# Value products evicted to SBUF in one step, their low half on GpSimd, one rotation buffer and convolution statistics one chunk earlier, in a two-layer decoder trunk

## The chip, the cores and the metric

The kernel runs on one core of a Trainium2 chip. The metric is the time of one execution on the device in microseconds. Before the change it is 650.95 us, the median of three runs (650.80, 650.95 and 651.51). The changed kernel is to be timed in the same way.

## What is computed

Two layers (DEPTH = 2) act on x of 256 positions by 1024 channels. In each layer one wide projection feeds a convolution branch and an attention branch. With one block of 256 keys the block-sparse attention is plain causal attention over 16 heads of 64.

```
u = x @ w_in + b_in
a_val, a_glu, a_z, q, k, v, b_z, g_a, g_b = jnp.split(u, SPLIT_POINTS, axis=-1)
h   = causal_depthwise_conv31(a_val * sigmoid(a_glu)) + conv_b
y_a = ((silu(layer_norm(h, cln_g, cln_b)) @ w_pw2) * silu(a_z)) @ w_proj_a
o   = softmax(causal(rope(q) / 8 @ rope(k).T)) @ v
y_b = (o * silu(b_z)) @ w_proj_b
out = (sigmoid(g_a) * y_a + sigmoid(g_b) * y_b) @ w_out
x   = layer_norm(ALPHA * x + out, ln_g, ln_b)
```

## The kernel before

**Numbers in two halves.** Every matrix and activation is kept as a high half (a rounded copy, written by ScalarE) and a low half (the rest, a subtraction). A product is high x high + high x low + low x high. All activations lie with channels on the partitions and the 256 positions along the free axis, except v and the last projection.

**The weight stream.** `STREAM` lists 52 weight tiles of 1 MB for each layer, in the order V, A_GLU and A_VAL by turns, B_Z, then the attention stage MID (Q, K, G_A by turns, then G_B), then A_Z, PB, PW2, PA, WO; each name has four tiles. `split_w` loads a tile (SP's queue), has ACT write its high half (line 120, four pieces) and POOL its low half (line 124, four pieces; a few tiles go to DVE). Raw, high and low tiles have three buffers each, and two tiles are prepared ahead.

**A gemm.** `gemm_a` uses one weight tile for two output chunks of 128 channels. A chunk is 8 matmuls of 512 columns (line 176: high weights on high and low activations side by side) and 8 of 256 columns (line 174: low weights). PSUM has three such buffers ("mm"). A chunk leaves by an ACT copy of the low product (`lw`, line 182 or 184), a DVE addition (line 187) and the evacuation that belongs to the projection. The order on PE is written out by hand (`manual_schedule`) in MID, A_Z and PB; a scheduler sets the order on the other engines, and in PW2 and PA on PE too. Where `gemm_a` calls a hook inside a chunk, it does so after its eighth matmul.

**Attention, in MID.** The rotation (`rope`, lines 429 to 440) is four DVE instructions for each Q or K tile. A pair p of heads (0 to 7) goes through three steps that hooks place between the matmuls of later gemms:

- `att_scores`: scores into one PSUM tile s (line 451), mask and maxima on DVE (457 to 459), exponentials on ACT (461 and 464), the reciprocal on DVE (466), the scaling on ACT (468 writes p0, 469 writes p1).
- `att_trans`: six transposes on PE into two PSUM tiles of the pool `ptp`, ta and tb (lines 477, 478, 479). The pool has two buffers, so that ta of pair p takes the buffer of ta of pair p-1, and tb that of tb. ACT copies them out (482, 483).
- `att_av`: the value product is written into the free half of tb (lines 491, 494). Then, lines 495 to 498:

```
g = ps[:, :S]
nc.vector.scalar_tensor_tensor(g, g, bias(V, p), bz[:, p, :], op0=ALU.add, op1=ALU.mult)
nc.scalar.activation(og[:, p, :], g, AF.Copy)
nc.vector.tensor_tensor(ol[:, p, :], g, og[:, p, :].bitcast(F32), op=ALU.subtract)
```

Here g is still the PSUM tile tb: DVE adds the bias and multiplies by the gate in place, ACT writes the high half, DVE the low half, and only then is tb free for the next pair's line 479.

**Convolution.** 31 taps for each of 8 channel tiles run on DVE in the background (line 381), some after every gemm chunk (`background`); line 386 sums the tiles for the mean. Its layer norm is placed by the constants `CM`, `CV` and `CB`: `hook_az` calls `cln_mu` after chunk `CM` of A_Z (matmul of line 542 on PE, subtraction 545, squares 546); `ev_pb` calls `cln_var` after chunk `CV` of PB (the sums 533 to 535, matmul 551, then the reciprocal root 554 to 559), and after chunk ct the tiles in `CB[ct]` go through `cln_b` (564 to 568), which writes hc, the input of PW2.

Of the kernel before, what the change touches and what calls it, by code (L numbers as in the profile page):

```python
# [10 lines left out]
F32 = mybir.dt.float32  # L11
# [4 lines left out]
ALU = mybir.AluOpType  # L16
# [4 lines left out]
S = 256  # L21
D = 1024
P = 128
# [8 lines left out]
NEG = -1e30  # L32
EARLY = 6
NH2 = 2
CM = 5.0
CV = 1
CB = [[], [], [0, 1], [2, 3], [4, 5], [6, 7], [], []]
KE = 7
KN = 5
L1, L2, L3 = 2.5, 5.5, 7.0  # L40
# [8 lines left out]
A_VAL, A_GLU, A_Z, Q, K, V, B_Z, G_A, G_B, PW2, PA, PB, WO = range(13)  # L49
# [21 lines left out]
def decoder_trunk(ctx: ExitStack, tc: tile.TileContext, a, out):  # L71
    nc = tc.nc
# [8 lines left out]
    tmp = ctx.enter_context(tc.tile_pool(name="tmp", bufs=2))  # L81
# [6 lines left out]
    def u_f32(name, shape=(P, KT, S)):  # L88
        return unit.tile(list(shape), F32, tag="u", name=name)

    def u_pair(name):

        both = pair.tile([P, KT, 2, S], F32R, tag="p", name=name)
        return both[:, :, 0, :], both[:, :, 1, :], both
# [51 lines left out]
    def background(n):  # L146
        with tc.high_priority(offset=-LATE):
            for _ in range(min(n, len(conv_ops))):
                conv_ops.pop(0)()
# [153 lines left out]
    for l in range(DEPTH):  # L303
# [3 lines left out]
        def bias(b, ct):  # L307
            return pc[:, b * KT + ct : b * KT + ct + 1]
# [104 lines left out]
        bz = u_f32(f"bz{l}")  # L413
# [9 lines left out]
        og, ol, op_ = u_pair(f"og{l}")  # L423
        qk = {}

        def ev_qk(b):
            return lambda j, ps: rope(b, j, ps)

        def rope(b, j, ps):
            u = tmp.tile([P, 2, S], F32, tag="t1", bufs=2, name=f"u_{l}_{b}_{j}")  # L430
            t2 = tmp.tile([P, 2, S], F32, tag="t2", bufs=1, name=f"t2_{l}_{b}_{j}")
            r0 = 2 if b == Q else 0
            cosb = rt[:, r0 : r0 + 1, :].to_broadcast([P, 2, S])
            sinb = rt[:, r0 + 1 : r0 + 2, :].to_broadcast([P, 2, S])
            nc.vector.tensor_tensor(u, ps, sinb, op=ALU.mult)
            nc.vector.stream_shuffle(t2, u, SWAP)
            nc.vector.tensor_tensor(ps, ps, cosb, op=ALU.mult)
            r = tmp.tile([P, 2, S], F32, tag="qk", bufs=4, name=f"r_{l}_{b}_{j}")
            nc.vector.tensor_tensor(r, ps, t2, op=ALU.add)
            qk[b, j] = r  # L440
# [45 lines left out]
        def att_av(p):  # L486
            pa, pb, tb = st[p]
            ps = tb[:, 2:, :].rearrange("p a q -> p (a q)")
            for e in range(2):
                hs = slice(p * P + e * HD, p * P + e * HD + HD)  # L490
                nc.tensor.matmul(ps[e * HD : e * HD + HD, :S], v[:, 0, hs], pa[:, e, :], start=True, stop=False)  # L491
            for e in range(2):
                hs = slice(p * P + e * HD, p * P + e * HD + HD)
                nc.tensor.matmul(ps[e * HD : e * HD + HD, P:S], v[:, 1, hs], pb[:, e, :], start=False, stop=True)
            g = ps[:, :S]
            nc.vector.scalar_tensor_tensor(g, g, bias(V, p), bz[:, p, :], op0=ALU.add, op1=ALU.mult)
            nc.scalar.activation(og[:, p, :], g, AF.Copy)
            nc.vector.tensor_tensor(ol[:, p, :], g, og[:, p, :].bitcast(F32), op=ALU.subtract)

        def ev_gate(b, dst):  # L500
            def f(ct, o):
# [5 lines left out]
        for n, (b, j) in enumerate(MID):  # L507
            if b == K:
                at = 2 * n + 1
                for p in (2 * j, 2 * j + 1):  # L510
                    for d, f in ((L1, att_scores), (L2, att_trans), (L3, att_av)):
                        plan.setdefault(at + d, []).append((f, p))
                    at += 3
# [34 lines left out]
        def cln_var():  # L548
            f = fold(cln["sq"], cln["sq"])
            vp = cvp.tile([P, 2, S], F32, tag="cv", name=f"cvar{l}")  # L550
            nc.tensor.matmul(vp[:, 0, :], ones, f, start=True, stop=True)
            u = tmp.tile([P, S], F32, tag="g", bufs=2, name=f"cu{l}")
            y = vp[:, 1, :]
            nc.scalar.activation(u, vp[:, 0, :], AF.Sqrt, bias=eps)
            nc.vector.reciprocal(y, u)
            nc.scalar.activation(u, y, AF.Square)
            nc.vector.tensor_scalar(vp[:, 0, :], vp[:, 0, :], EPS, None, op0=ALU.add)
            nc.vector.scalar_tensor_tensor(u, u, -0.5, vp[:, 0, :], op0=ALU.mult, op1=ALU.mult)
            nc.vector.scalar_tensor_tensor(y, u, 1.5, y, op0=ALU.add, op1=ALU.mult)
            cln["r"] = y  # L560

        def cln_b(ct):
            z = ptp.tile([P, 512], F32, tag="pt", name=f"z{l}_{ct}")[:, :S]
            nc.vector.tensor_tensor(z, cv[:, ct, :], cln["r"], op=ALU.mult)
            nc.scalar.activation(z, z, AF.Silu, bias=pc[:, C_LB + ct : C_LB + ct + 1],  # L565
                                 scale=pc[:, C_LG + ct : C_LG + ct + 1])
            nc.scalar.activation(hc[0][:, ct, :], z, AF.Copy)
            nc.vector.tensor_tensor(hc[1][:, ct, :], z, hc[0][:, ct, :].bitcast(F32), op=ALU.subtract)

        def ev_pb(ct, o):  # L570
            nc.vector.scalar_tensor_tensor(gb[:, ct, :], gb[:, ct, :], 1.0, o, op0=ALU.add, op1=ALU.mult)  # L571
            if ct == CV:
                hc.extend(u_pair(f"hc{l}"))
                cln_var()
            for q in CB[ct]:
                cln_b(q)

        def hook_az(c, j):
            if 2 * j + c == CM:
                background(len(conv_ops))  # L580
                cln_mu()
# [22 lines left out]
        mh, ml, _ = u_pair(f"mg{l}")  # L604
# [166 lines left out]
```

## Time and profile before

| | before |
|---|---|
| median of three runs | 650.95 us |
| the profiled execution | 650.61 us |
| its span, first to last instruction | 648.8 us |
| PE (matmuls) busy | 633.8 us |
| DVE busy | 485.3 us |
| ACT busy | 438.4 us |
| POOL busy | 487.6 us |
| granted TensorE clock, mean | 0.997 |

The profiled execution is 1.8 us longer than its span, and 0.34 us shorter than the median. PE is TensorE's matmuls, PEld its weight loads, DVE VectorE, ACT ScalarE, POOL GpSimd, SP the engine that issues the weight loads from HBM. A PE that is busy all the time can still lose time: the ends of its matmuls are modelled and overlap, so the distance between two starts tells more than the busy time.

### The profile page before, as it was taken

The page shows a single profiled execution, that of the slowest core. Times are in us where ns is not written, and L with a number is a line of the kernel's source. Part 1 is how long each engine was busy: PE and PEld are TensorE (multiplying, and loading weights), DVE is VectorE, ACT ScalarE, POOL GpSimd, SP SyncE. Part 2 cuts the span into 40 slices and gives each one's busy share as a digit, 9 for nine tenths or more (in the row PEclk, how much of TensorE's full clock was granted, in tenths as well). Part 3 has the DMA queues.
Part 4 walks back from the last instruction along what each step waited for, and adds up shares of the span by engine and source line. Part 5 has one row for each costly group of instructions (what it writes and reads, how often), then busy time and mean ns, then how long its engine had stood idle before and what let it go on. Part 6 is the DMA issues. An engine that isn't in the chain of part 4 may idle for free.

```text
span 648.8 us, 10605 instructions
## 1 busy us (share of the span) xinstructions
PE 633.8 (98%) x3662; PEld 542.2 (84%) x3662; DVE 485.3 (75%) x1129; ACT 438.4 (68%) x1019; POOL 487.6 (75%) x387
## 2 busy tenths in 40 slices
PE   8999999999999999999999999999999999999995
PEld 6888888887878888988788888888877888889884
DVE  4668989999998666445840899899999886664556
ACT  4675665887778689656527566668777787885641
POOL 0099999777566898989628999996677589999851
PEclk9999999999999999999999999999999999999998
DMA  8966555443333564555653555554433344555401
GB/s 272 351 235 251 190 196 195 162 162 131 131 129 131 195 250 155 201 179 195 254 195 116 209 195 204 191 190 154 173 131 130 130 146 179 195 186 191 175 33 66
DMA packets 19191, 116.06 MB, mean 179 GB/s; under 512 B 2113, under 2 KB 3393, under 8 KB 6209
## 3 DMA queue, kind: packets, MB, share of 16 engines
q1 hardware_dynamic: 18416, 114.72, 49.2%
q10 hardware_dynamic: 720, 0.66, 0.4%
q8 instruction: 29, 0.48, 0.3%
q14 instruction: 26, 0.20, 0.1%
HBM read 114.32 MB, written 1.05 MB: 178 GB/s over the span
## 4 chain that ended last, share of the span: by engine, by line
PE 83%; ACT 7%; DVE 4%; DMA 3%; POOL 1%; issue 1%; POOLq 0%; ACTq 0%
PE mm L176 43%; PE mm L174 23%; PE wo L210 3%; PE v L210 3%; ACT hi L120 3%; PE v L340 3%; PE s L451 2%; PE mm L171 2%; DMA raw<-w 1%; DMA xf<-xT 1%; PE tb L491 1%; POOL lo L124 1%; ACT z L565 1%; PE tb L479 1%; ACT s L461 1%
## 5 line engine op out<-in xcount | busy, mean ns | idle before, releaser
L124 POOL TENSOR_TENSOR lo<-raw,hi 128x512 fp32r<-128x512 f32 x380 | 485.8, 1315 | 138.4 <-ACT hi L120 133.6
L176 PE MATMUL mm<-x,hi 128*128 128x512 f32 x1024 | 263.8, 395 | 0.0
L120 ACT ACTIVATE hi<-raw 128x512 fp32r<-128x512 f32 x412 | 235.7, 629 | 23.3 <-DMA raw<-w 15.5
L176 PEld LDWEIGHTS mm<-x,hi 128*128 128x128 f32 x1024 | 184.0, 189 | 34.4 <-issue 2.4
L381 DVE SCALAR_TENSOR_TENSOR cv<-h,pc,cv 128x256 f32<-128x256 f32 x464 | 196.4, 481 | 0.2
L174 PEld LDWEIGHTS mm<-x,lo 128*128 128x128 f32 x1024 | 139.5, 190 | 11.2
L174 PE MATMUL mm<-x,lo 128*128 128x256 f32 x1024 | 147.5, 284 | 0.0
L187 DVE TENSOR_TENSOR mm<-mm,lw 128x256 f32<-128x256 f32 x172 | 73.5, 430 | 80.6 <-ACT lw L182 51.7
L182 ACT ACTIVATE lw<-mm,pc 128x256 f32<-128x256 f32 x128 | 61.4, 480 | 86.5 <-PE mm L176 86.3
L176 PE MATMUL mm<-og,hi 128*128 128x512 f32 x128 | 33.1, 396 | 0.0
L210 PE MATMUL wo<-hi,mg 128*128 128x512 f32 (+1 forms) x144 | 32.7, 368 | 0.1
L176 PE MATMUL mm<-ah,hi 128*128 128x512 f32 x128 | 32.4, 393 | 0.0
L124 DVE TENSOR_TENSOR lo<-raw,hi 128x512 fp32r<-128x512 f32 x32 | 25.6, 844 | 7.4 <-ACT hi L120 7.4
L210 PEld LDWEIGHTS wo<-hi,mg 128*128 128x128 f32 x144 | 25.2, 189 | 5.2 <-DVE mg L610 0.9
L184 ACT ACTIVATE lw<-mm 128x256 f32<-128x256 f32 x44 | 16.8, 386 | 16.7 <-PE mm L176 15.8
L176 PEld LDWEIGHTS mm<-og,hi 128*128 128x128 f32 x128 | 23.3, 189 | 4.1
L176 PEld LDWEIGHTS mm<-ah,hi 128*128 128x128 f32 x128 | 23.1, 189 | 4.0
L176 PE MATMUL mm<-hc,hi 128*128 128x512 f32 x96 | 25.1, 397 | 0.5 <-DVE gb L571 0.5
L176 PEld LDWEIGHTS mm<-hc,hi 128*128 128x128 f32 x96 | 17.3, 189 | 4.7 <-ACT z L565 1.3
L174 PEld LDWEIGHTS mm<-og,lo 128*128 128x128 f32 x128 | 17.5, 191 | 1.2
L174 PEld LDWEIGHTS mm<-ah,lo 128*128 128x128 f32 x128 | 17.5, 190 | 1.2
L461 ACT ACTIVATE s<-s,nm 128x256 f32<-128x256 f32 x32 | 14.1, 441 | 5.9 <-DVE nm L459 5.9
(139 smaller groups left out, 711.0 us busy)
## 6 DMA issues: line engine op xcount, KB each, us to landing
raw<-w SPq DMA_DIRECT2D x101, 1024.0 KB, 4.8
raw<-w SPq DMA_DIRECT2D x8, 256.0 KB, 5.2
rows<-pr SPq DMA_DIRECT2D x4, 512.0 KB, 6.1
raw<-w SPq DMA_DIRECT2D x2, 512.0 KB, 8.3
xs<-x SPq DMA_DIRECT2D x1, 1024.0 KB, 7.0
out<-xs SPq DMA_DIRECT2D x3, 256.0 KB, 2.0
xf<-xT ACTq DMA_DIRECT2D x4, 128.0 KB, 5.5
xf<-xT SPq DMA_DIRECT2D x2, 256.0 KB, 4.4
```

Source lines behind the costliest of these rows:

```text
L120: nc.scalar.activation(hi[:, ks, :], raw[:, ks, :], AF.Copy)
L124: eng.tensor_tensor(lo[:, ks, :], raw[:, ks, :], hi[:, ks, :].bitcast(F32), op=ALU.subtract)
L171: nc.tensor.matmul(ps[:, 0, :], (wl if q == 2 else wh)[:, k, cs], both[:, k, int(q == 1), :], start=(n == 0), stop=(n == len(seq) - 1))
L174: nc.tensor.matmul(ps[:, 0, :], wl[:, k, cs], both[:, k, 0, :], start=False, stop=False)
L176: nc.tensor.matmul(ps, wh[:, k, cs], both[:, k, :, :], start=(n == 0), stop=(k == KT - 1))
L182: nc.scalar.activation(t, low, AF.Identity, bias=pcs[0][:, b * KT + ct : b * KT + ct + 1])
L184: nc.scalar.activation(t, low, AF.Copy)
L187: nc.vector.tensor_tensor(kept[:, c if b in (Q, K) else 0, :], o, t, op=ALU.add)
L210: nc.tensor.matmul(o, (xl if q == 1 else xh)[:, kk, ts], (wl if q == 2 else wh)[:, k, cols], start=(kk == 0 and n == 0), stop=(kh == 1 and ...
L340: nc.tensor.matmul(o[t], (xl if r == 1 else xh)[:, kk, ts], (wl if r == 2 else wh)[:, k, :], start=(kk == 0 and r == 0), stop=(kk == 7 and ...
L381: r = nc.vector.scalar_tensor_tensor(dst, src, w, acc[:, c, :], op0=ALU.mult, op1=ALU.add)
L461: nc.scalar.activation(s1[:, e, :], s1[:, e, :], AF.Exp, bias=nm[:, 2 + e : 3 + e], accum_out=sm[:, 2 + e : 3 + e])
```

## The change

The diff is whole:

```
@@ -32,9 +32,9 @@
 NEG = -1e30
 EARLY = 6
 NH2 = 2
-CM = 5.0
-CV = 1
-CB = [[], [], [0, 1], [2, 3], [4, 5], [6, 7], [], []]
+CM = 4.0
+CV = 0
+CB = [[], [0, 1], [2, 3], [4, 5], [6, 7], [], [], []]
@@ def rope(b, j, ps):
-            u = tmp.tile([P, 2, S], F32, tag="t1", bufs=2, name=f"u_{l}_{b}_{j}")
+            u = tmp.tile([P, 2, S], F32, tag="t1", bufs=1, name=f"u_{l}_{b}_{j}")
@@ def att_av(p):
-            g = ps[:, :S]
-            nc.vector.scalar_tensor_tensor(g, g, bias(V, p), bz[:, p, :], op0=ALU.add, op1=ALU.mult)
+            g = tmp.tile([P, S], F32, tag="og", bufs=2, name=f"og{l}_{p}")
+            nc.vector.scalar_tensor_tensor(g, ps[:, :S], bias(V, p), bz[:, p, :], op0=ALU.add, op1=ALU.mult)
             nc.scalar.activation(og[:, p, :], g, AF.Copy)
-            nc.vector.tensor_tensor(ol[:, p, :], g, og[:, p, :].bitcast(F32), op=ALU.subtract)
+            nc.gpsimd.tensor_tensor(ol[:, p, :], g, og[:, p, :].bitcast(F32), op=ALU.subtract)
```

The first instruction of `att_av` now writes an SBUF tile g with two buffers, so it alone reads the value product out of tb. The low half (line 498) is a GpSimd instruction. The product u in the rotation has one buffer. The mean and the variance of the convolution's layer norm, and the tiles of hc, are each placed one chunk (16 matmuls) earlier. The scheduler answers with another order on all engines but SP. Line numbers stay as they were.

**ACT, at the softmax of pair 5 in layer 0** (s is the scores' tile, lw a gemm's low product, hi a weight tile's high half, p_0 the probabilities, ga a gate). Before:

```order
L120 ACTIVATE hi_2106<-raw_2000 128x512 x3
L461 ACTIVATE s_5_2057,sm_5_2063<-s_5_2057,nm_5_2062 128x256
L120 ACTIVATE hi_2106<-raw_2000 128x512
L461 ACTIVATE s_5_2057,sm_5_2063<-s_5_2057,nm_5_2062 128x256
L182 ACTIVATE lw_0_2133<-mm_0_2116,pc_181 128x256
L464 ACTIVATE s_5_2057,sm_5_2063<-s_5_2057,nm_5_2062 128x128 x2
L468 ACTIVATE p_0_5_2066<-s_5_2057,rc_5_2064 128x128
L469 ACTIVATE p_0_5_2065<-s_5_2057,rc_5_2064 128x256
L468 ACTIVATE p_0_5_2066<-s_5_2057,rc_5_2064 128x128
L469 ACTIVATE p_0_5_2065<-s_5_2057,rc_5_2064 128x256
L502 ACTIVATE ga_1118<-mm_0_2116 128x256
L182 ACTIVATE lw_1_2165<-mm_1_2148,pc_181 128x256
```

Now:

```order
L120 ACTIVATE hi_2110<-raw_2004 128x512 x4
L182 ACTIVATE lw_0_2137<-mm_0_2120,pc_181 128x256
L461 ACTIVATE s_5_2061,sm_5_2067<-s_5_2061,nm_5_2066 128x256 x2
L464 ACTIVATE s_5_2061,sm_5_2067<-s_5_2061,nm_5_2066 128x128 x2
L502 ACTIVATE ga_1118<-mm_0_2120 128x256
L182 ACTIVATE lw_1_2170<-mm_1_2153,pc_181 128x256
L468 ACTIVATE p_0_5_2070<-s_5_2061,rc_5_2068 128x128
L469 ACTIVATE p_0_5_2069<-s_5_2061,rc_5_2068 128x256
L468 ACTIVATE p_0_5_2070<-s_5_2061,rc_5_2068 128x128
L469 ACTIVATE p_0_5_2069<-s_5_2061,rc_5_2068 128x256
```

The copies of the low products (line 182), each of which waits for the end of a gemm chunk on PE, stand ahead of the exponentials and of the scaling where they stood behind them.

**DVE, ahead of the eviction of pair 4 (line 496), layer 0** (rc is the reciprocal of pair 5's sums, fold the sum for the mean; the brackets name the semaphores that an instruction waits on). Before:

```order
L466 RECIPROCAL rc_5_2064<-sm_5_2063 128x4 [waits Activation_49]
L187 TENSOR_TENSOR mm_0_2116<-mm_0_2116,lw_0_2133 128x256 [waits PE_49]
L381 SCALAR_TENSOR_TENSOR h<-h,pc_181,cv_2_1188 128x256 [waits DVE_49] x2
L386 TENSOR_TENSOR fold_819<-h,fold_819 128x256 [waits DVE_49]
L377 TENSOR_SCALAR cv_3_1858<-h,pc_181 128x256 [waits DVE_49]
L386 TENSOR_TENSOR fold_819<-h,fold_819 128x256 [waits DVE_49]
L496 SCALAR_TENSOR_TENSOR tb_4_2046<-tb_4_2046,pc_181,bz_853 128x256 [waits PE_49]
L377 TENSOR_SCALAR cv_3_1858<-h,pc_181 128x256
L187 TENSOR_TENSOR mm_1_2148<-mm_1_2148,lw_1_2165 128x256 [waits Activation_49]
L498 TENSOR_TENSOR og_1120<-tb_4_2046,og_1120 128x256 [waits Activation_49]
```

Now:

```order
L187 TENSOR_TENSOR mm_0_2120<-mm_0_2120,lw_0_2137 128x256 [waits Activation_49]
L381 SCALAR_TENSOR_TENSOR h<-h,pc_181,cv_2_1188 128x256 [waits DVE_49]
L466 RECIPROCAL rc_5_2068<-sm_5_2067 128x4 [waits Activation_49]
L381 SCALAR_TENSOR_TENSOR h<-h,pc_181,cv_2_1188 128x256 [waits DVE_49]
L386 TENSOR_TENSOR fold_819<-h,fold_819 128x256 [waits DVE_49]
L377 TENSOR_SCALAR cv_3_1861<-h,pc_181 128x256 [waits DVE_49]
L386 TENSOR_TENSOR fold_819<-h,fold_819 128x256 [waits DVE_49]
L496 SCALAR_TENSOR_TENSOR og_4_2145<-tb_4_2050,pc_181,bz_853 128x256 [waits PE_49,Pool_49]
L377 TENSOR_SCALAR cv_3_1861<-h,pc_181 128x256
L187 TENSOR_TENSOR mm_1_2153<-mm_1_2153,lw_1_2170 128x256 [waits Activation_49]
```

Line 496 writes og_4 instead of tb_4 and waits on POOL's semaphore too (from pair 2 on), since its buffer must have been read two pairs before; one convolution tap and the addition of line 187 stand ahead of line 466 instead of behind it, and line 498 is gone from DVE.

**PE, at the start of PW2, layer 0** (mm_0 and mm_1 are the two chunks of the first tile, hc the normalized convolution). Before:

```order
L176 MATMUL mm_0_3072<-hc_2829,hi_2924 128x512 x6
L176 MATMUL mm_1_3095<-hc_2829,hi_2924 128x512 x4
L176 MATMUL mm_0_3072<-hc_2829,hi_2924 128x512
L174 MATMUL mm_0_3072<-hc_2829,lo_2925 128x256 x8
L176 MATMUL mm_0_3072<-hc_2829,hi_2924 128x512
L176 MATMUL mm_1_3095<-hc_2829,hi_2924 128x512 x3
L174 MATMUL mm_1_3095<-hc_2829,lo_2925 128x256 x8
L176 MATMUL mm_1_3095<-hc_2829,hi_2924 128x512
```

Now:

```order
L176 MATMUL mm_0_3080<-hc_2816,hi_2942 128x512 x7
L174 MATMUL mm_0_3080<-hc_2816,lo_2943 128x256 x8
L176 MATMUL mm_0_3080<-hc_2816,hi_2942 128x512
L176 MATMUL mm_1_3103<-hc_2816,hi_2942 128x512 x7
L174 MATMUL mm_1_3103<-hc_2816,lo_2943 128x256 x8
L176 MATMUL mm_1_3103<-hc_2816,hi_2942 128x512
```

Four matmuls of the second chunk no longer stand inside the first chunk. Elsewhere on PE: the matmuls that filled the time between the transposes 478 and 479 change their number (pair 2: two before, none now; pair 4: two and one; pair 6: five before, now one ahead of each of its two lines 478), and lines 542 and 551 stand one chunk earlier. On POOL the 16 new subtractions stand between the low halves of weight tiles or inside one. SP's order is the same.

## Rows read from the trace of the kernel before

**Rows 1.** The page, part 1: busy us of each engine (share of the span) x instructions.

```profile
PE 633.8 (98%) x3662; PEld 542.2 (84%) x3662; DVE 485.3 (75%) x1129; ACT 438.4 (68%) x1019; POOL 487.6 (75%) x387
```

**Rows 2.** View of the waits of PE: line <- releaser: us in total, times, longest.

```profile
PE tb L479 <- DVE og L498: 3.2, 4, 0.8
...
PE mm L176 <- DVE gb L571: 0.5, 2, 0.2
```

**Rows 3.** The chain that ended last, in order of time: start, us, what.

```profile
32.20 1.84 PE mm L176 x8
```

**Rows 4.** Timeline around pair 3, layer 0: start, us, engine, line, op, [idle before <- releaser].

```profile
156.82 0.49 DVE L496 SCALAR_TENSOR_TENSOR tb<-tb,pc,bz 128x256 f32<-128x256 f32 x1
...
157.82 0.27 PE L477 MATMUL ta<-ident,p 128*128 128x128 f32 x1
...
157.93 0.27 PE L478 MATMUL ta<-ident,p 128*128 128x128 f32 x1
...
158.41 0.42 DVE L498 TENSOR_TENSOR og<-tb,og 128x256 fp32r<-128x256 f32 x1 [0.37 <-ACT og L497]
...
158.97 0.30 PE L479 MATMUL tb<-ident,p 128*128 128x128 f32 x1 [0.78 <-DVE og L498]
```

**Rows 5.** Timeline of PE at pair 5, layer 0.

```profile
181.07 0.27 PE L478 MATMUL ta<-ident,p 128*128 128x128 f32 x1
182.15 0.30 PE L479 MATMUL tb<-ident,p 128*128 128x128 f32 x1 [0.81 <-DVE og L498]
```

**Rows 6.** Timeline of PE at the start of PW2, layer 0.

```profile
255.20 1.54 PE L176 MATMUL mm<-hc,hi 128*128 128x512 f32 x6
256.98 1.51 PE L176 MATMUL mm<-hc,hi 128*128 128x512 f32 x5 [0.24 <-DVE gb L571]
258.33 1.11 PE L174 MATMUL mm<-hc,lo 128*128 128x256 f32 x8
```

**Rows 7.** Groups of instructions by line: xcount | busy us, mean ns | idle before.

```profile
L571 DVE SCALAR_TENSOR_TENSOR gb<-gb,mm 128x256 f32<-128x256 f32 x16 | 6.5, 415 | 0.2
...
L651 POOL TENSOR_TENSOR side<-side,rows 128x256 f32<-128x256 f32 x1 | 0.7, 723 | 0.5 <-ACT side L650 0.5
```

**Rows 8.** Timeline of POOL, three weight tiles of layer 0.

```profile
174.38 5.06 POOL L124 TENSOR_TENSOR lo<-raw,hi 128x512 fp32r<-128x512 f32 x4 [3.19 <-ACT hi L120]
180.81 5.00 POOL L124 TENSOR_TENSOR lo<-raw,hi 128x512 fp32r<-128x512 f32 x4 [1.38 <-ACT hi L120]
...
216.56 5.24 POOL L124 TENSOR_TENSOR lo<-raw,hi 128x512 fp32r<-128x512 f32 x4 [1.31 <-ACT hi L120]
```

**Rows 9.** Timeline of ACT ahead of the transposes of pair 5.

```profile
175.24 0.44 ACT L461 ACTIVATE s<-s,nm 128x256 f32<-128x256 f32 x1
...
175.69 0.62 ACT L120 ACTIVATE hi<-raw 128x512 fp32r<-128x512 f32 x1
...
176.66 0.48 ACT L182 ACTIVATE lw<-mm,pc 128x256 f32<-128x256 f32 x1
177.01 0.35 ACT L464 ACTIVATE s<-s,nm 128x128 f32<-128x128 f32 x1
```

**Rows 10.** Timeline of DVE, same stretch.

```profile
178.00 0.18 DVE L466 RECIPROCAL rc<-sm 128x4 f32<-128x4 f32 x1 [0.22 <-ACT s L464]
...
179.19 0.52 DVE L386 TENSOR_TENSOR fold<-h,fold 128x256 f32<-128x256 f32 x1
...
180.42 0.48 DVE L496 SCALAR_TENSOR_TENSOR tb<-tb,pc,bz 128x256 f32<-128x256 f32 x1
```

**Rows 11.** Timeline of PE at the transposes of pair 6.

```profile
193.18 1.40 PE L176 MATMUL mm<-x,hi 128*128 128x512 f32 x5
194.42 0.27 PE L479 MATMUL tb<-ident,p 128*128 128x128 f32 x1
```

**Rows 12.** Timeline of DVE at the end of the convolution.

```profile
219.91 2.17 DVE L386 TENSOR_TENSOR fold<-h,fold 128x256 f32<-128x256 f32 x2
...
227.03 1.22 DVE L545 TENSOR_TENSOR h<-h,cmu 128x1024 f32<-128x1024 f32 x1 [2.22 <-PE cmu L542]
```

## The prediction

> **What bounds the kernel now.** I read the page's busy times first: PE is busy 98% of the span, and no other engine over 75% [rows 1]. So only time that PE itself loses can be won. The view of PE's waits names where it loses any in both layers: four waits of line 479 for DVE's line 498, and two at line 176 for line 571 [rows 2]. These sums understate the loss, because a matmul's modelled end overlaps the idle time behind it; I take the distance between starts instead. The unit is 0.23 us for a matmul of 512 columns, 1.84 us for eight [rows 3].
>
> At pair 3 the transposes 477 and 478 start 0.11 us apart, but 479 starts 1.04 us behind 478 [rows 4]: 0.93 us are lost. The reader should see why. Line 479 writes tb, which the pair before still holds. DVE's line 496 was through with the value product at 157.31 (156.82 and 0.49), but tb stays taken until line 498 has read it too, at 158.83; PE goes on 0.14 us later. Pair 5 shows the same with 1.08 - 0.11 = 0.97 us [rows 5]. Four such waits [rows 2] make 2 x (0.93 + 0.97) = **3.8 us**. The other pairs show none in the list.
>
> At the start of PW2, six matmuls from 255.20 should be followed by the next at 256.58; it starts at 256.98, 0.40 late. Five more from there should end at 258.13, and line 174 starts at 258.33, 0.20 late [rows 6]. The second of these is the wait for the last tiles of hc, the first the wait for a PSUM buffer, which the order with four matmuls of the second chunk brings forward. Two layers make 2 x 0.60 = **1.2 us**.
>
> **The change part by part.**
>
> *Eviction.* tb is free after line 496. On the old times that is 157.31 + 0.14 = 157.45 at pair 3, where PE wants it at 158.04: no wait, by 0.59 us. At pair 5 it is 180.42 + 0.48 + 0.14 = 181.04 [rows 10] against 181.18: no wait, but by 0.14 only. What line 496 costs when it writes SBUF is not shown; line 571, of the same form and size with an SBUF output, takes 0.42 us [rows 7] against 0.48 or 0.49 now. So its cost lies between 0.07 less and no change, and I take no change.
>
> *The new order takes part of the margin back.* At pair 5, ACT's copy of line 182 starts at 176.66 and ends its turn at 177.01; now two exponentials of line 461, 0.45 us each with their read of the sums, follow it, and then the two of line 464, which end about 1.0 us after their start [rows 9, 10]. So line 466 on DVE moves from 178.00 to about 177.01 + 0.90 + 1.0 = 178.9. Behind it stands line 496, 2.42 us later before [rows 10]; line 187 and one tap no longer stand between. Three full instructions and the short reciprocal filled the 1.19 us from 178.00 to 179.19, so two of them are worth about 0.7 us (an estimate from these rows). Line 496 then starts at 178.9 + 1.72 = 180.6, and tb is free at 181.24, 0.06 us late. At pair 3 one exponential moves behind the copy, which takes about 0.5 of the 0.59 us. I set 0.1 us for each of the four waits, 0.4 us given back; the bounds are 0 and, if everything came 0.5 us later, 2.4 us (4 x 0.6).
>
> *Pair 6.* Before, five matmuls filled the time ahead of 479; they took 194.42 - 193.18 = 1.24 us, 0.09 more than 5 x 0.23 [rows 11], the price of changing back to transposes. Now there are two such changes, 0.09 more in each layer. ACT's new order also puts line 497 and one more line 120 ahead of pair 6's scaling, so its probabilities come nearly when PE asks for them; I take 0.15 us, bounded by 0 and the length of the two instructions, about 1 us (0.62 for line 120 [rows 9]). Together 0.24 x 2 = 0.5 us given back. Pairs 2 and 4 lose fillers and nothing else.
>
> *The subtraction on GpSimd.* The nearest row is GpSimd's two-input instruction of the same size, line 651 at 0.72 us [rows 7], against DVE's 0.42 [rows 4]. Eight in each layer fit the gaps of 1.38 and 3.19 us that POOL spends between weight tiles in the attention stage [rows 8], waiting for ACT; its result is wanted only in PB. On the path it costs 0. If the cover were gone, it would add at most 16 x 0.72 = 11.5 us of POOL's time, and the low halves of the weights would be late next. DVE is relieved of 16 x 0.42 us, which PE does not feel otherwise. The Trainium skill, GPSIMD Engine Reference, section 4.1 (engine selection), speaks against this part: two-input elementwise work belongs on VectorE, GpSimd being about twice as slow. Rows 4 and 7 agree in direction (0.72 against 0.42), and by that rule, were each subtraction on the path, the sum would lose 16 x 0.30 = 4.8 us, more than it wins; the gaps of rows 8 say that it is not.
>
> *One buffer for u.* Lines 435 and 436 that write and read u follow one another on DVE, so the next write comes after the read in any case: 0.
>
> *Convolution statistics.* The fold ends at 222.08 (219.91 and 2.17), and DVE's line 545 waited until 227.03 for the matmul of line 542 [rows 12]. A chunk takes about 2.8 us (1.84 and half of that again for the 256 columns), so placing 542 a chunk earlier uses 2.8 of 4.95 us: PE does not wait for the fold. All that follows moves up by about a chunk, more than the 0.20 us by which hc was late, and the order no longer asks early for the PSUM buffer. The whole 1.2 us go; the bounds are 0 and 1.2.
>
> **The sum**, against the profiled execution's 650.61 us: -3.8 + 0.4 + 0.5 - 1.2 = -4.1, so 646.5 us. The median before is 0.34 above that execution; I say **646.6 us**. About 0.2% (1.3 us) is what a measurement of this kernel can tell from no change. PE's saving carries to the end, since the weight stream waits for buffers that PE frees. The best by the bounds is -5.0, 645.6.
>
> **Rivals.**
>
> 1. *The softmax becomes the wait.* With the copies of line 182 ahead of the exponentials and the scaling, the transposes wait for p0 and p1, and line 496 behind line 466, by about 0.6 us instead of 0.1. For it: the order in both places; the margin of 0.14 at pair 5. Against it: the copies wait for a chunk that ends eight matmuls ahead of the transposes, so both move together. Half the 3.8 us returns: 646.6 + 1.9 = 648.5.
>
> 2. *GpSimd slows DVE just ahead of line 496.* The trace shows line 386 at 0.52 us when POOL's tile ends at 179.44 during it, and 1.09 each (2.17 for two) at 219.91, when POOL works through to 221.80 [rows 8, 10, 12]. Were POOL busy under the two folds ahead of pair 4's line 496, that line would come 2 x 0.6 = 1.2 us later, and pair 5's wait would return in both layers: 646.6 + 2.4 = 649.0. Against it: in the new order too, no weight tile and no subtraction is due there between 179.4 and the next tile. The Trainium skill, GPSIMD Engine Reference, section 1 (specifications), has it as a rule: GpSimd's SBUF interfaces are shared with VectorE, with contention where a VectorE instruction has two SBUF inputs. The trace agrees, with 0.52 against 1.09 us for line 386.
>
> 3. *No change.* tb's release is not what the transposes wait for, because ACT's probabilities come just as late; then 3.8 us stay, and the rest nets 1.2 - 0.5: about 650. Against it: rows 4 show PE released 0.14 us behind line 498, and nothing else.
>
> 4. *Slower: the ring of two buffers.* Line 496 of pair p waits for POOL's line 498 of pair p-2, which stands in POOL's queue behind weight tiles; behind line 496 on DVE stand the evacuations of the gemms, and PE waits for tb. It decides once POOL is later than two pairs, 23.6 us (156.82 to 180.42 [rows 4, 10]). If the 12 waiting instructions came 0.6 us too late for PE each, 7.2 us would be lost: 646.6 + 7.2 = 653.8. Against it: a tile is 5.06 us and a gap at most 3.19 [rows 8], so POOL should be done in under 9.
>
> **Chances.** Forecast 0.66 (its own range 645.0 to 647.9), softmax 0.11, DVE slowed 0.07, no change 0.10, the ring 0.06. The first three are faster by over 0.2%: 0.84; same 0.10; slower 0.06. The range runs from 645.0 to 649.6: it takes in the bounds of the eviction and of pair 6, and rivals 1 and 2.
>
> **What would show it.** Right: no wait of 479 for DVE among PE's waits, 478 to 479 at 0.11 to 0.3 us in pairs 3 and 5; eight matmuls of PW2 with no gap; line 498 on POOL near 0.7 us. Wrong: starts of 477 or 478 held by ACT's 468 or 469, line 479 held by line 496, DVE waiting for POOL, or PE held at line 542 or 551.

## The result, and the profile after

The changed kernel takes **646.0 us** (median of six runs, 645.69 to 646.17), the kernel before in the same session 650.88 (650.53 to 651.51). The ratio is 0.9923, with a 95% interval of 0.9913 to 0.9933, so 4.4 to 5.7 us are won. Forecast were 646.6 us and a range of 645.0 to 649.6. The profiled execution took 645.89 us, 4.72 less than the one before.

The span of the changed kernel is 644.1 us. Part 1 of its page (busy us of each engine, share of the span, instructions), against [rows 1]:

```profile
PE 632.8 (98%) x3662; PEld 542.6 (84%) x3662; DVE 480.9 (75%) x1113; ACT 439.8 (68%) x1019; POOL 497.2 (77%) x403
```

PE is the bound as before. DVE gave 16 instructions to POOL. What changed is in the view of PE's waits (line, releaser: us in total, times, longest), against [rows 2]:

```profile
PE wps L248 <- ACT warm L245: 2.7, 1, 2.7
PE xt L671 <- DVE xs L657: 0.3, 1, 0.3
PE v L340 <- DVE x L263: 0.3, 1, 0.3
```

These are all the rows of the view, and the kernel before has the same three beside those of [rows 2]. The waits of line 479 for line 498 and of line 176 for line 571 are gone, and no other has come in their place. The timeline of PE in the changed kernel (start, us, engine, line) shows the three places: pair 3 [rows 4] and pair 5 [rows 5], pair 6 [rows 11], and the start of PW2 [rows 6].

```profile
158.09 0.27 PE L478 MATMUL ta<-ident,p 128*128 128x128 f32 x1
158.20 0.27 PE L479 MATMUL tb<-ident,p 128*128 128x128 f32 x1
...
180.15 0.27 PE L477 MATMUL ta<-ident,p 128*128 128x128 f32 x1
180.26 0.27 PE L478 MATMUL ta<-ident,p 128*128 128x128 f32 x1
180.37 0.27 PE L479 MATMUL tb<-ident,p 128*128 128x128 f32 x1
...
180.90 0.81 PE L451 MATMUL s<-r,r 64*128 64x256 f32 x6
...
191.23 0.27 PE L477 MATMUL ta<-ident,p 128*128 128x128 f32 x1
...
192.50 0.70 PE L451 MATMUL s<-r,r 64*128 64x256 f32 x4
...
253.45 1.77 PE L176 MATMUL mm<-hc,hi 128*128 128x512 f32 x7
255.06 1.11 PE L174 MATMUL mm<-hc,lo 128*128 128x256 f32 x8
```

In pairs 3 and 5 line 479 follows 478 by 0.11 us, where it took 1.04 and 1.08. Pair 5's transposes and the step to the next scores take 0.75 us (180.15 to 180.90). Pair 6's take 1.27: the same 0.75, two matmuls of 0.23 between them, and 0.06 more. At PW2 the seven matmuls from 253.45 take 7 x 0.23 us, line 174 follows at 255.06, and nothing is late.

### The profile page after: what moved, and what is told of

It reads as the page before. It is cut to its first block, busy times and chain, and to the rows that moved or that the text cites. A ratio compares the mean times of both kernels' runs of the same rounds, so it can differ in the third digit from the quotient of the medians.

```text
span 644.1 us, 10614 instructions
## 1 busy us (share of the span) xinstructions
PE 632.8 (98%) x3662; PEld 542.6 (84%) x3662; DVE 480.9 (75%) x1113; ACT 439.8 (68%) x1019; POOL 497.2 (77%) x403
## 3 DMA queue, kind: packets, MB, share of 16 engines
HBM read 114.32 MB, written 1.05 MB: 179 GB/s over the span
## 4 chain that ended last, share of the span: by engine, by line
PE 93%; DMA 3%; DVE 2%; POOL 1%; issue 0%; ACT 0%; POOLq 0%; ACTq 0%
PE mm L176 49%; PE mm L174 26%; PE wo L210 3%; PE v L210 3%; PE v L340 3%; PE s L451 2%; PE mm L171 2%; DMA raw<-w 2%; PE tb L491 1%; DMA xf<-xT 1%; POOL lo L124 1%; PE ta L478 1%; PE ta L477 1%; PE tb L479 1%; PE tb L494 1%; DVE lo L124 0%
## 5 line engine op out<-in xcount | busy, mean ns | idle before, releaser
L184 ACT ACTIVATE lw<-mm 128x256 f32<-128x256 f32 x44 | 17.5, 398 | 14.9 <-PE mm L176 14.4
L174 PE MATMUL mm<-ah,lo 128*128 128x256 f32 x128 | 17.9, 283 | 0.0
```

What stands on the lines that cost most here:

```text
L174: nc.tensor.matmul(ps[:, 0, :], wl[:, k, cs], both[:, k, 0, :], start=False, stop=False)
L184: nc.scalar.activation(t, low, AF.Copy)
```

## The experiments

The parts of the change were run apart first. The order of the scheduler shifts with every edit, so each kernel was read in its own trace. "The kernel before" is always its runs on the same chip in the same session.

### u1: one buffer for the rotation's product

```diff
-            u = tmp.tile([P, 2, S], F32, tag="t1", bufs=2, ...)
+            u = tmp.tile([P, 2, S], F32, tag="t1", bufs=1, ...)
```

> The kernel before with one buffer for u and nothing else; the order on every engine stays the same. Theory (lines 435 and 436 follow one another on DVE, so the second buffer was never used): 650.9, within 0.3 us. Rival (the write of u waits for the read to be through its pipe, some 0.1 us in each of 16 rotations, and PE feels it): up to 652.

Measured: 650.87 us against 650.85, ratio 0.9999 (0.9990 to 1.0008). The second buffer bought no time; giving it up only pays for the memory of og.

### order_only, cmv_only, cb_only: the convolution's statistics

All three start from the kernel before and set constants alone: order_only all three, the others a part.

```diff
-CM = 5.0
-CV = 1
+CM = 4.0
+CV = 0
```

```diff
-CB = [[], [], [0, 1], [2, 3], [4, 5], [6, 7], [], []]
+CB = [[], [0, 1], [2, 3], [4, 5], [6, 7], [], [], []]
```

> The kernel before with the three constants of the statistics alone. Theory A (hc is ready, and PE meets no wait at PW2): -1.2 us, 649.7; the waits of line 479 stay. Rival (the wait for hc is won at PW2 and given back at the next one, since the weights pace PE): 650.9, no change.

> The kernel before with lines 542 and 551 one chunk earlier (CM and CV) and CB as it was, so that hc's tiles come in the old places. PE's order at the start of PW2 loses the four matmuls that ask early for a PSUM buffer. Theory (the 0.40 us of a layer is the order, the 0.20 us is hc): -0.8, 650.0. Rival (both are the order's): -1.2, 649.7. Rival (hc comes late all the same): 650.9.

> The kernel before with CB alone one slot earlier; PE's order at the start of PW2 stays (six matmuls, then four of the second chunk). Theory: hc is ready, so the 0.20 us of a layer goes, and the 0.40 us for the PSUM buffer stays: -0.4, 650.4. Rival (what waits for the buffer waits for hc's evacuation too): -1.2, 649.7.

Measured: order_only 649.82 us, ratio 0.9986 (0.9977 to 0.9994); cmv_only 649.64, ratio 0.9984 (0.9975 to 0.9992); both against 650.85 and 650.84. cb_only 650.70, ratio 0.9999 (0.9991 to 1.0008). So the two constants that place lines 542 and 551 are worth 1.0 to 1.2 us, and CB nothing that can be measured. The timelines tell why. In cmv_only, DVE's last low half of hc and PE's start of PW2:

```profile
255.20 0.41 DVE L568 TENSOR_TENSOR hc<-z,hc 128x256 fp32r<-128x256 f32 x1
...
255.29 1.77 PE L176 MATMUL mm<-hc,hi 128*128 128x512 f32 x7
```

The same places in cb_only:

```profile
256.04 1.54 PE L176 MATMUL mm<-hc,hi 128*128 128x512 f32 x6
257.83 1.51 PE L176 MATMUL mm<-hc,hi 128*128 128x512 f32 x5 [0.24 <-DVE gb L571]
...
258.36 0.76 DVE L568 TENSOR_TENSOR hc<-z,hc 128x256 fp32r<-128x256 f32 x2 [0.35 <-ACT hc L567]
```

And hc's last tiles in the kernel before, where PW2 starts at 255.20 [rows 6]:

```profile
257.52 0.76 DVE L568 TENSOR_TENSOR hc<-z,hc 128x256 fp32r<-128x256 f32 x2 [0.35 <-ACT hc L567]
```

With CB alone hc's last low halves start 2.32 us behind PW2 (258.36 - 256.04), exactly as before (257.52 - 255.20). PE's order keeps six matmuls ahead of four of the next chunk, and the gap stays. With CM and CV the last low half starts 0.09 us ahead of PW2, in time for the last matmuls of its chunk, the order has seven matmuls and there is no gap. The place of lines 542 and 551, not CB, sets when hc is ready. My split into 0.40 us for the order and 0.20 for hc was not put to the test: I had expected cmv_only to leave hc in its old place, but it moved hc as well, and cb_only moved neither. The two went or stayed together.

### cm3: one chunk earlier still

```diff
-CM = 4.0
+CM = 3.0
```

> The changed kernel with line 542 one chunk (2.8 us) earlier still. The fold ends at 220.3 in the changed kernel, and PE would reach line 542 at about 219.0. Theory (the prediction's: the margin is 2.8 of 4.95 us, so it holds one chunk, not two): PE waits about 1.3 to 1.5 us for the fold in each layer, 648.6 to 649.0. Rival (the taps are drawn earlier too, and the fold with them): 646.0.

Measured: 648.70 us, ratio to before 0.9970 (0.9958 to 0.9983), 2.7 us above the changed kernel, as the theory had it. The timeline of cm3, PE and then DVE:

```profile
218.74 0.39 PE L176 MATMUL mm<-x,hi 128*128 128x512 f32 x1
220.28 0.70 PE L542 MATMUL cmu<-fold,ones 128*128 128x256 f32 x2 [1.14 <-DVE fold L386]
...
218.07 2.15 DVE L386 TENSOR_TENSOR fold<-h,fold 128x256 f32<-128x256 f32 x2
```

Line 542 could start at 218.97 (218.74 and 0.23) and starts at 220.28, behind the fold: 1.31 us in each layer. One chunk is the most that this margin holds.

### evict_pool and evict_dve: the eviction, with the subtraction on GpSimd and on DVE

Both are the changed kernel with the old CM, CV and CB; evict_dve also leaves line 498 on DVE.

```diff
-            nc.gpsimd.tensor_tensor(ol[:, p, :], g, og[:, p, :].bitcast(F32), op=ALU.subtract)
+            nc.vector.tensor_tensor(ol[:, p, :], g, og[:, p, :].bitcast(F32), op=ALU.subtract)
```

> The same with line 498 on GpSimd; statistics in their old places. Theory A: as with line 498 on DVE, 647.2, the two within 0.3 us of each other. Theory B: here the whole gain of 3.7 comes, 647.2, and line 498 on DVE gives at most half. Theory C (the new order of DVE, ACT and PE gives back what the prediction took, 0.9 us): 648.0 in both.

> Line 496 writes SBUF (two buffers, paid for by one buffer for u), but line 498 stays on DVE, and the convolution statistics keep their old places. Theory A (only the early release of tb pays): PE's waits of line 479 are gone, those of lines 174 and 176 at the start of PW2 stay; -3.7 us, so 647.2 (646.6 to 647.8). Theory B (what pays is that DVE is relieved of line 498): tb is free early, but line 496 or the softmax comes late behind line 498 on DVE, and half or more of the 3.7 stays: 649 or above.

Measured: evict_pool **647.33 us**, ratio 0.9943 (0.9931 to 0.9956): the 3.5 us of the eviction. evict_dve **659.29 us**, ratio 1.0125 (1.0111 to 1.0139): slower than before by 8.4 us, and by 12.0 than with GpSimd. I had taken the two to be equal. Theory B has the direction and not the place: line 498 is not what stands ahead of line 496. PE's waits in evict_dve:

```profile
PE tb L479 <- DVE og L496: 3.6, 2, 1.8
...
PE ta L477 <- ACT p L468: 2.2, 2, 1.1
```

One pair in each layer, pair 5, holds them all. To see why, follow it back in evict_dve's timeline from PE to DVE (lines 466, 386, 496) and from there to ACT (the copy of line 182, an exponential of line 464):

```profile
184.84 0.33 PE L479 MATMUL tb<-ident,p 128*128 128x128 f32 x1 [1.79 <-DVE og L496]
...
181.28 0.18 DVE L466 RECIPROCAL rc<-sm 128x4 f32<-128x4 f32 x1 [1.41 <-ACT s L464]
181.38 1.15 DVE L386 TENSOR_TENSOR fold<-h,fold 128x256 f32<-128x256 f32 x1
...
184.31 0.47 DVE L496 SCALAR_TENSOR_TENSOR og<-tb,pc,bz 128x256 f32<-128x256 f32 x1
...
179.56 0.47 ACT L182 ACTIVATE lw<-mm,pc 128x256 f32<-128x256 f32 x1 [0.92 <-PE mm L176]
179.93 0.33 ACT L464 ACTIVATE s<-s,nm 128x128 f32<-128x128 f32 x1
```

The same of ACT and DVE in evict_pool:

```profile
177.69 0.34 ACT L464 ACTIVATE s<-s,nm 128x128 f32<-128x128 f32 x1
...
178.85 0.47 ACT L182 ACTIVATE lw<-mm,pc 128x256 f32<-128x256 f32 x1 [0.42 <-PE mm L176]
...
178.19 0.18 DVE L466 RECIPROCAL rc<-sm 128x4 f32<-128x4 f32 x1
...
178.65 0.42 DVE L386 TENSOR_TENSOR fold<-h,fold 128x256 f32<-128x256 f32 x1
...
179.77 0.48 DVE L496 SCALAR_TENSOR_TENSOR og<-tb,pc,bz 128x256 f32<-128x256 f32 x1
```

In evict_pool ACT does both exponentials of line 464 ahead of the copy of line 182, which waits for a chunk of PE. In evict_dve the copy stands ahead of them and ACT waits for PE (0.92 us) with the softmax behind it. Line 466 comes at 181.28 instead of 178.19 and holds DVE, which is idle for 1.41 us; the scaling, at 181.92, is late for line 477. Being late, the two folds of line 386 now fall under POOL's tile (from 180.98 on) and take 1.15 and 1.04 us instead of 0.42. Line 496 is 4.5 us later than in evict_pool, and line 479 is late with it (PE's last matmul ahead of these transposes is only 0.7 us later, at 180.97 against 180.25). These are rivals 1 and 2 of the prediction together, brought on by the order that came out with line 498 on DVE.

### dve_late and dve_100: the same instructions on DVE, in other places of its queue

Both are evict_dve with line 498 at a lower priority: 150 steps (LATE, as the taps have it) and 100.

```diff
-            nc.vector.tensor_tensor(ol[:, p, :], g, og[:, p, :].bitcast(F32), op=ALU.subtract)
+            with tc.high_priority(offset=-LATE):
+                nc.vector.tensor_tensor(ol[:, p, :], g, og[:, p, :].bitcast(F32), op=ALU.subtract)
```

> Made to explain the 659.3 us of the kernel that evicts to SBUF and keeps line 498 on DVE (statistics in their old places). Here line 498 stays on DVE too, but with the low priority of the convolution's taps, so that it no longer stands ahead of the softmax's line 459 and of lines 466 and 496 in DVE's queue; DVE does the same work. Theory D (what cost 8.4 us is where line 498 puts the other instructions in DVE's queue, not DVE's load): the loss goes, about 647.3, as with line 498 on GpSimd. Theory E (DVE is nearly full in the attention stage, and 16 x 0.42 us more ahead of the same deadlines is what it can't carry): 655 or above. Between, some of each.

Measured: 650.41 us, ratio to before (651.09) 0.9990 (0.9981 to 1.0000). Of 12.0 us 8.9 are back with line 498 still on DVE, and 3.1 are not. DVE's line 498 (L499 here) of pair 1, the same of pair 2 with line 496 of pair 4 behind it, and PE's line 479 of pair 5:

```profile
168.37 1.28 DVE L499 TENSOR_TENSOR og<-og,og 128x256 fp32r<-128x256 f32 x1
...
180.84 0.41 DVE L499 TENSOR_TENSOR og<-og,og 128x256 fp32r<-128x256 f32 x1
...
181.51 0.47 DVE L496 SCALAR_TENSOR_TENSOR og<-tb,pc,bz 128x256 f32<-128x256 f32 x1
...
182.12 0.30 PE L479 MATMUL tb<-ident,p 128*128 128x128 f32 x1 [1.25 <-DVE og L496]
```

The softmax is in time here (line 466 starts at 177.99), but the put-off subtraction now stands close ahead of line 496 of two pairs later, which writes the buffer that it reads. At 168.37 it is stretched to 1.28 us (the last section shows by what); PE hardly feels that at pair 4, where four matmuls stand between lines 478 and 479. At pair 5 line 479 waits, and starts 1.52 us behind line 478 instead of 0.11. Once in each layer, that makes 2.8 of the 3.1 us. The next kernel puts the subtraction away from both deadlines:

> Eviction to SBUF, line 498 on DVE, statistics in their old places, with a priority between the two tried: line 498 now stands among the taps, right behind a pair's softmax deadlines, and lines 457 to 459, 466 and 496 stand in nearly the order that they have with line 498 on GpSimd. DVE does the same work as in both kernels with line 498 on DVE (659.3 and 650.4 us). Theory D (the place in DVE's queue, and the long line 498 just ahead of line 496, were what cost time): 647.3, within 0.6, as with GpSimd. Theory E (DVE's load itself): 649 or above, with line 479 waiting for line 496 at pairs 4 or 5.

Measured: 654.84 us, ratio 1.0074 (1.0060 to 1.0088). Theory D's number falls and theory E's fits; whether its reason does too, the trace tells. Line 498 does stand among the taps, but ACT's order is again the bad one, as its rows and DVE's say:

```profile
178.66 0.48 ACT L182 ACTIVATE lw<-mm,pc 128x256 f32<-128x256 f32 x1 [0.70 <-PE mm L176]
...
180.39 0.18 DVE L466 RECIPROCAL rc<-sm 128x4 f32<-128x4 f32 x1 [1.18 <-ACT s L464]
180.48 1.15 DVE L386 TENSOR_TENSOR fold<-h,fold 128x256 f32<-128x256 f32 x1
```

The copy waits for PE ahead of line 464, and the rest follows as in evict_dve. Is DVE's load behind it? The table of busy time by stretch answers for 170 to 182 us, one row for each kernel (stretch, length, then PE, PEld, DVE, ACT, POOL busy, granted clock, DMA share, GB/s): evict_pool,

```profile
170.00:182.00 12.00, 12.00 (x82) 9.84 (x79) 11.89 (x30) 9.48 (x27) 7.17 (x7) 1.00 0.41 154
```

and dve_100:

```profile
170.00:182.00 12.00, 10.86 (x69) 8.55 (x67) 10.35 (x24) 8.54 (x25) 6.96 (x6) 1.00 0.36 124
```

DVE is fuller in the kernel that loses nothing (11.89 of 12 us), and dve_100's DVE has 1.65 us to spare in the stretch ahead of PE's waits: it is not short of time there, and theory E's reason finds no support.

One thing the three kernels share, and I had not reckoned with it: line 498 costs DVE more than the 0.42 us that I took. Its group in the kernel before and in evict_dve (count, then busy us and mean ns):

```profile
L498 DVE TENSOR_TENSOR og<-tb,og 128x256 fp32r<-128x256 f32 x16 | 6.7, 422 | 2.7 <-ACT og L497 2.5
L498 DVE TENSOR_TENSOR og<-og,og 128x256 fp32r<-128x256 f32 x16 | 15.6, 974 | 2.1 <-ACT og L497 1.3
```

With one input in PSUM it took 0.41 to 0.43 us every time. With both inputs in SBUF it takes 0.41 to 1.58 us, on average 0.97 in evict_dve, 0.91 in dve_late and 0.90 in dve_100, longer than the 0.74 us on GpSimd. The total is nearly the same in the three (15.6, 14.6 and 14.4 us), so it is not what sets them apart: three orders of the same instructions gave 659.3, 650.4 and 654.8 us. What stays open is whether any order brings the last 3.1 us back: a kernel with line 498 on DVE and every queue otherwise exactly as in evict_pool was not tried, so whether DVE could carry the longer subtraction at no cost is not shown.

### pool3, pool8 and ring1: GpSimd's cover, and the ring

pool3 and pool8 are the changed kernel with line 498 issued three and eight times (the same values each time, written to the same place); ring1 gives og one buffer instead of two.

```diff
-            nc.gpsimd.tensor_tensor(ol[:, p, :], g, og[:, p, :].bitcast(F32), op=ALU.subtract)
+            for _ in range(8):
+                nc.gpsimd.tensor_tensor(ol[:, p, :], g, og[:, p, :].bitcast(F32), op=ALU.subtract)
```

> The changed kernel with line 498 issued three times on GpSimd, 16 x 2 x 0.74 = 23.7 us more POOL work, 11.8 in each attention stage, where POOL is idle for 23.5 of 97 us. Theory (GpSimd's subtraction is covered by its waits for ACT): 646.0, within 0.5. Rival (it delays the weight tile that stands behind it, and PE waits for that): each layer loses some us, 648 to 655.

> The same issued eight times: 8 x 7 x 0.74 = 41 us more in each attention stage, more than the 23.5 idle. Theory (cover of 23.5 us plus the 6 to 10 us by which the low halves lead their use): 8 to 18 us late in each layer, 662 to 682. If the time stays at 646, POOL's idle time is larger than the profile shows.

> The changed kernel with one buffer for og instead of two, the same order on every engine: line 496 of a pair waits for GpSimd's line 498 of the pair before. Theory (line 498 is done 6 us or more ahead of the next line 496): 646.0, within 0.3. Rival of the prediction (the ring binds): DVE waits for POOL at line 496, and the waits of line 479 come back, 648 or above.

Measured, against 651.09 before: pool3 645.96 us, ratio 0.9926 (0.9910 to 0.9943); ring1 646.26, ratio 0.9924 (0.9909 to 0.9938). Neither differs from the changed kernel. pool8 took 687.27, ratio 1.0554 (1.0539 to 1.0570), 41 us above the changed kernel and over the top of what was expected. Its waits of PE and of DVE, and its row of busy time for 200 to 250 us (the stretches' columns as above):

```profile
PE mm L174 <- POOL lo L124: 21.3, 19, 2.5
```

```profile
DVE og L496 <- POOL og L499: 5.9, 2, 2.9
```

```profile
200.00:250.00 50.00, 39.20 (x180) 31.05 (x179) 28.27 (x56) 25.59 (x57) 48.44 (x49) 0.87 0.31 111
```

POOL is full (48.4 of 50 us), PE waits for low halves, DVE waits at line 496 for the ring, and PE's clock is granted at 0.87 on average. The waits are half of the 41 us. An estimate for the clock from this row: 39.2 us of PE's busy time at 0.87 are about 34 at full clock, so 5 us in layer 0. My sum had left out the clock; the rest, some 10 of the 41 us if layer 1 loses as much to the clock, I did not trace. So the subtraction on GpSimd is covered threefold and not eightfold.

## Why the prediction was right, and where not

- **What bounds the kernel** held: PE's own gaps, and the whole gain is read off them.
- **Eviction**, 3.8 us: right. The two traces give 1.04 - 0.11 and 1.08 - 0.11 in layer 0, and 1.05 and 1.06 less 0.11 in layer 1, 3.8 in all; evict_pool measured 3.5. Line 496 with an SBUF output takes 479 ns on average, as taken. Line 498 on GpSimd:

```profile
L498 POOL TENSOR_TENSOR og<-og,og 128x256 fp32r<-128x256 f32 x16 | 11.8, 739 | 2.3 <-ACT og L497 2.3
```

- **"The new order takes part of the margin back"**, 0.4 us: mis-sized, it measured nothing. DVE's rows of the changed kernel, against [rows 10]:

```profile
177.96 0.18 DVE L466 RECIPROCAL rc<-sm 128x4 f32<-128x4 f32 x1
...
179.54 0.48 DVE L496 SCALAR_TENSOR_TENSOR og<-tb,pc,bz 128x256 f32<-128x256 f32 x1
```

  Line 466 is 2.30 us ahead of line 478 (180.26), before it was 3.07: 0.77 later, where I took 0.9. Line 496 follows 1.58 us behind it, where I took 1.72. tb is free at 179.54 + 0.48 + 0.14 = 180.16, 0.21 us ahead of 180.37, not 0.06 late. At pair 3 the margin grew as well, from 0.59 to 0.90 us (line 496 at 156.68, line 479 at 158.20).
- **"Pair 6"**, 0.5 us given back: mis-sized, it measured about 0.1. The two fillers cost 0.06 us in each layer. By the same measure the five of before had cost 0.01 and not 0.09: from line 478 (193.15) to line 479 (194.42) PE took 1.27 us, which is 0.11 + 5 x 0.23 + 0.01. The scaling was in time: the list of PE's waits names no line 468 or 469.
- **The statistics**, 1.2 us: right in size (order_only 1.0, cmv_only 1.2), wrong in its parts: CB does nothing, and no run parts the 0.20 us for hc from the 0.40 us for the order. The margin was smaller than the 4.95 us taken: that is counted to DVE's line 545, but PE's line 542, which must not come ahead of the fold, started at 226.40, 4.3 us behind the fold's end at 222.08. It holds one chunk of 2.8 us all the same, and not two (cm3).
- **The subtraction on GpSimd**, 0: right as a cost (0.74 us, and pool3 shows room for two more). "DVE is relieved ... which PE does not feel otherwise" was wrong as a reading of the part: with the eviction, each of three ways to keep it on DVE came out 3.1 to 12.0 us above evict_pool, and most of the 8.9 us between the three came with the order. The rule that I weighed (the Trainium skill, GPSIMD Engine Reference, section 4.1) agrees with the trace where nothing disturbs DVE, 0.74 us on GpSimd and 0.41 on DVE; on average over the 16 the measurement goes the other way once both inputs are in SBUF, 0.74 on GpSimd and 0.90 to 0.97 on DVE. The Trainium skill, GPSIMD Engine Reference, section 1 (specifications), states that GpSimd has no access to PSUM; no run here shows it, and GpSimd alone, without the eviction, was not tried.
- **The rivals.** "No change" fell with the waits of line 479, which went and left no wait for ACT in their place. Softmax and slowed DVE did not come in this kernel and did in evict_dve and dve_100, by the mechanisms described. The ring did not bind, not even with one buffer; it did once POOL was full (pool8).

The two terms that held make 5.0 us, the medians 4.9 and the profiled executions 4.7; the interval covers all three. The stated 646.6 lies 0.25 us below the prediction's own sum: 646.5 is the sum for the profiled execution, and with the 0.34 us by which the median is higher it gives 646.85. Against that the miss is 0.85 us, and it is the two terms given back (0.9 us, of which about 0.1 came), each within its stated bounds; that the stated figure missed by only 0.6 is luck.

No version tried here beats the changed kernel: pool3, ring1 and it are alike; cm3, evict_pool and all the others are slower.

## What to carry to other kernels

When a PSUM tile holds up the next user, ask which reader lets go of it last, and let the first reader move it to SBUF; what follows can then go to any engine with time to spare, and "spare" is measured by issuing the work several times. An instruction that stays can change its length by the move: here line 498 on DVE went from 0.42 to 0.90 us and more once both its inputs were in SBUF. Where a scheduler sets the queues, an instruction moved off an engine changes the order on the others too: read the new order at the next deadline, and above all whether a copy that waits for PE has come to stand ahead of the exponentials. A part that costs nothing may still be the one without which the rest loses, as line 498 on GpSimd was in the orders tried here.

## What the runs showed of the hardware that I had not expected

**A DVE instruction that collides waits for the end of the GpSimd instruction.** DVE's line 386 takes 0.42 us with POOL idle (evict_pool at 178.65) and 1.15 in dve_100 at 180.48, where POOL works from 180.08 on. POOL's row there:

```profile
180.08 2.67 POOL L124 TENSOR_TENSOR lo<-raw,hi 128x512 fp32r<-128x512 f32 x2 [0.74 <-ACT hi L120]
```

The first of these two, 1.27 us long, ends at 181.35, and line 386 at 181.63, 0.28 us behind it: DVE waited for the whole POOL instruction. The second ends at 182.75, and the next line 386 (182.00, 1.03 us) again 0.28 us behind it. The Trainium skill, SBUF — State Buffer, section on its two separate sides, has this as an exclusive lock: whichever starts first keeps the shared ports for its whole instruction, and the other blocks. The trace agrees, with those 0.28 us. It also means that a DVE instruction made late can meet a collision that it had escaped: in evict_dve 3.1 us of delay at line 466 became 4.5 at line 496.

The same explains why line 498 became longer on DVE. In the kernel before, with the PSUM tile tb as one input, it took 0.42 us at 158.41 [rows 4] in the midst of a POOL tile (157.66 to 162.67); with both inputs in SBUF it takes 1.28 us in dve_late at 168.37, under a POOL tile that started at 165.55.

**A stall that costs more than its length.** In evict_dve PE stood for 1.11 and 1.79 us at pair 5, and in the stretch from 182 to 190 us the granted clock is 0.79 on average, between the levels of 1.2 and 2.4 GHz (1.00). In dve_100 the two waits are 1.11 and 1.34 us in both layers. In layer 0 the clock stays at 1.00 from 182 to 190 us; in layer 1 it is 0.79 from 500 to 508 us. The rows of evict_dve and of dve_100, and in dve_100 PE's line 479 of pair 5 and the first matmul of the gemm chunk after next, in layer 0 and in layer 1:

```profile
182.00:190.00 8.00, 5.82 (x27) 4.63 (x28) 6.78 (x16) 4.40 (x13) 4.21 (x4) 0.79 0.43 167
```

```profile
500.00:508.00 8.00, 6.42 (x29) 5.15 (x30) 6.55 (x16) 4.48 (x12) 4.27 (x4) 0.79 0.38 130
```

```profile
183.49 0.33 PE L479 MATMUL tb<-ident,p 128*128 128x128 f32 x1 [1.34 <-DVE og L496]
...
188.66 0.39 PE L176 MATMUL mm<-x,hi 128*128 128x512 f32 x1
...
502.24 0.33 PE L479 MATMUL tb<-ident,p 128*128 128x128 f32 x1 [1.34 <-DVE og L496]
...
508.95 0.39 PE L176 MATMUL mm<-x,hi 128*128 128x512 f32 x1
```

The same matmuls take 5.17 us in layer 0 and 6.71 in layer 1, so the lower clock cost 1.5 us behind waits of 2.45 us in all. In evict_dve they take 6.69 and 6.68 us in the two layers, so some 3 of its 12.0 us are the clock's. Why the same two waits lowered the clock in one layer of dve_100 and not in the other, no run here shows.
